# A decoder trunk's attention: quotients of two query tiles together, rotary addition on GpSimd, four PSUM banks for the cross attentions' last sums

## The chip, the cores and the metric

The kernel runs on one core of a Trainium2 chip. The metric is the device time of one execution in microseconds (us), the median of several runs.

## The reference

The program is two layers of a decoder trunk on 512 tokens of width 1024, in float32. In the stages that the change touches the reference computes:

```python
def diff_attention(x, ...):                 # layer 0: 8 heads
    q, k, v = split(x @ w_qkv, 3)           # per head two queries and two keys of 64, a value of 128
    q, k = rope(q), rope(k)
    lam = exp(sum(lq[0] * lk[0])) - exp(sum(lq[1] * lk[1])) + lam_init
    s = (q @ k.T) * 64 ** -0.5              # two score maps per head, causal mask
    p = softmax(where(mask, s, min))
    a = p[0] - lam * p[1]
    o = a @ v
    o = o * rsqrt(mean(o * o) + eps) * subln_g * (1 - lam_init)
    return o.reshape(S, H * 128) @ w_o
...
x = layer_norm(alpha * x + diff_attention(x, ...))
x = layer_norm(alpha * x + memory_cross_attention(x, mem, wq, wkv, wo))
```

Each layer is: a half-step SwiGLU network, a token mixer (layer 0: differential attention; layer 1: a pooling mixer), cross attention with 4 heads to 256 memory tokens, and a second SwiGLU network, each followed by a layer norm. In `rope` the halves of a head are rotated: x1 · cos − x2 · sin and x2 · cos + x1 · sin.

## The kernel before, in words

Every large product is made as three products of a float32 value's rounded part and rest (`mm3`, L201 to L203, named hi·hi, hi·lo and lo·hi here). To split a tile, ScalarE copies the rounded part (L114, tiles named `wh`, `a`, `xh`) and VectorE subtracts it (L115, `wl`, `a`, `xl`). PSUM has pairs of banks: `mm` for projections and last sums (`self.mm`), and `px`, `py`, `yz`, which `self.aux` takes in turn unless a pair is named. A bank comes free when the last reader has read it.

**The differential attention** (layer 0) is two programs that run woven into each other. `da_main` makes for each of the 8 heads the query and key projections (and values for two heads at once), and after each projection `da_rope` (L947 to L953): a shuffle of the projection on VectorE (L949), a product with the cosine on VectorE (L950), a product with the signed sine on GpSimd (L951), and the addition of both on VectorE (L952). Then the query is split (L962 ScalarE, L963 VectorE), or the key (L976 and L978 ScalarE, L977 VectorE). `da_side` goes through 32 steps, 8 heads by 4 query tiles of 128. Step s makes the scores of its tile, transposes the map of step s − 2, multiplies the map of step s − 3 with the values, and after a head's last tile scales and transposes the output. `weave` hands `da_side` a turn for each GAP of 900 ns of projection matmuls and starts a head's scores only LEAD of 6000 ns after its key.

For query tile i of a head `da_scores` makes two score maps of 128 × 128(i + 1) on TensorE (L991, L992), adds the mask and finds the row bound on VectorE (L996), and takes the exponential on ScalarE with the row sums as a second output (L997, sums in `sd`). Then VectorE makes the reciprocal of the second sum (L1000, `rc`), the factor −lam · sum0 / sum1 (L1001, `cf`) and the combination p0 + cf · p1 (L1002), the *quotient* in this text. The map stays unnormalised; the row norm of the output takes the first sum in.

`da_turn` transposes the combined map on TensorE (L479, `pt`), and L114 and L115 split it to `a`. `da_out` multiplies `a` with the values (L1022, L1023); every second tile ScalarE copies one half of the sum (L1027), VectorE adds the other (L1028), and ScalarE sums the squares of the two tiles (L1031). After a head's last tile GpSimd makes the row factor `f`: two small products of the first sums (L1038, L1039), the sum of squares added (L1040), and a power of −0.5 (L1041). ScalarE scales the four output tiles by it (L1047).

**The end of a cross attention** is `to_tokens`: 8 sums of 128 × 512 (`ps`, 4 heads' parts, L201 to L203) in the order `LAST`, each in the next of the two `mm` banks. VectorE adds each to the residual (L397) and so frees the bank. After a token tile's second half `ln_token` makes the layer norm: the mean (L406), the squares on ScalarE (L419), variance and its power on GpSimd (L420, L421), and two passes on VectorE (L423, L425); `turn_late` then transposes the tile for the next stage (L479) in between the last sums.

The order of the instructions on each engine is not written out. The program's scheduler lays it down ahead of the run, engine by engine, from the order of the calls and the data that they need; each engine then goes through its list and waits where an input or a buffer is missing.

Of the kernel before, what the change touches and what calls it, by code (L numbers as in the profile page):

```python
# [13 lines left out]
ALU = mybir.AluOpType  # L14
# [3 lines left out]
P = 128  # L18
D = 1024
S = 512  # L20
NT = S // P
# [5 lines left out]
ALPHA = (2 * DEPTH) ** 0.25  # L27
# [72 lines left out]
def drain(units):  # L100
    for _ in units:
        pass


class Trunk:
# [375 lines left out]

    def to_tokens(self, parts, w, k0, kn, first, last, scale, homes=(None, None)):

        nc = self.nc
        ws = [None, None]
        for half, t in LAST if last else sorted(LAST):
            c, o = slice(half * S, (half + 1) * S), slice(t * P, (t + 1) * P)
            if t == 0:
                ws[half] = self.rows(w, k0, kn, half * S, homes[half])
            ps = self.mm("ps")  # L490
            for k in range(kn):
# [454 lines left out]
    def da_rope(self, ps):  # L946
        nc = self.nc  # L947
        t1, t2 = self.tmp("rt"), self.tmp("rt")
        nc.vector.stream_shuffle(t2, ps, [(i + 16) % 32 for i in range(32)])  # L949
        nc.vector.tensor_tensor(t1, ps, self.ropeC, ALU.mult)  # L950
        nc.gpsimd.tensor_tensor(t2, t2, self.ropeS, ALU.mult)  # L951
        nc.vector.tensor_tensor(t1, t1, t2, ALU.add)  # L952
        return t1  # L953
# [27 lines left out]
    def da_scores(self, st, i):  # L981
# [3 lines left out]
        qi, kn = slice(i * P, n), slice(0, n)  # L985
        mx, rc, cf = self.small("mx"), self.small("rc", (P, 1)), self.small("cf", (P, 1))
        sm = st["sm"][:, i]
# [6 lines left out]
        for m in range(2):  # L994
# [4 lines left out]
            )  # L999
        nc.vector.reciprocal(rc, sm[:, 1:2])  # L1000
        nc.vector.scalar_tensor_tensor(cf, sm[:, 0:1], self.nlam, rc, ALU.mult, ALU.mult)  # L1001
        nc.vector.scalar_tensor_tensor(p[0], p[1], cf, p[0], ALU.mult, ALU.add)  # L1002
        st["p", i] = p[0]

# [72 lines left out]
    def da_side(self):  # L1077
# [4 lines left out]
        self.nc.sync.dma_start(self.mask[:, S - P :], self.a["mask"])  # L1082
        for s in range(n + LS + 2):
            h, i = divmod(s, NT)
            if s < n:
# [314 lines left out]
    def xa(self, layer, ln):  # L1400
# [6 lines left out]
        homes = [[lambda: self.pair("q")] * 4, [kv] * 4]  # L1407
        drain(self.to_tokens(self.oT[4:], self.a["xa_wo"][layer], 4, 4, False, True, ALPHA, homes))

# [69 lines left out]
    def mixer(self, layer, ln):  # L1479
        if layer == 0:  # L1480
            bufs = dict(low=4, rt=2, a=4, p=4, o=1, qk=8, _x=0, v=4, oT=11, mask=1)
            with self.other_pools(), self.phase_pool(("v", "v"), "rt", **bufs):
# [60 lines left out]
```

## Time and profile before

| | |
|---|---|
| runs | 1938.06, 1935.68, 1937.65 us |
| median | 1937.65 us |
| the profiled execution | 1939.3 us |
| its span, first to last instruction | 1937.5 us |
| granted TensorE clock in it | 0.999 |
| instructions | 32405 |
| read from and written to memory | 274.15 MB, 4.20 MB |

In the profile PE is TensorE's matmul and PEld its weight load, DVE is VectorE, ACT ScalarE, POOL GpSimd. A row of the timeline has the start and the duration of an instruction in us, its engine and line, what it writes and reads, and in brackets the idle time of the engine before it and what ended it. A row of the waits has the total, the number and the longest of all waits of one kind. A row of the groups has the total us and the mean ns of one instruction, then the idle time just before them. The differential attention's woven part lies between about 375 and 560 us, the last sums of layer 0's cross attention around 735 to 756 us.

### The profile page before, as it was taken

To read this page: it belongs to the slowest core of one execution; us is meant where nothing else is said; L and a number is where in the kernel's file an instruction comes from. 1 tells how busy PE (TensorE), PEld (TensorE's weight loads), DVE (VectorE), ACT (ScalarE), POOL (GpSimd) and SP (SyncE) were. 2 spreads that over 40 slices of the span, in tenths; PEclk is the share of its full clock that TensorE was granted. 3 is DMA by queue.
4 is the path that set the end of the run, shared out by engine and by line. 5 is a ranking of instruction groups with operands and counts; after the bars stand their busy time and mean duration, and the time that the engine had idled before them with its cause. 6 is when DMAs were issued, how large, how long until landed. Compare 5 with 4: busy or idle time off the path is not lost.

```text
span 1937.5 us, 32405 instructions
## 1 busy us (share of the span) xinstructions
PE 1904.6 (98%) x12988; PEld 1738.8 (90%) x12988; DVE 1555.8 (80%) x2262; ACT 1015.8 (52%) x1543; POOL 334.8 (17%) x318
## 2 busy tenths in 40 slices
PE   9999999999999999999999999999999999999998
PEld 8999998888888888999998999999898889999996
DVE  7988887888867558788888988898886568898886
ACT  6655553567755435645554655455454436555552
POOL 2212121111211002211220321212110013211211
PEclk9999999999999999999999999999999999999999
DMA  9878772322126326978784688877444337777861
GB/s 253 198 173 185 171 145 66 92 67 87 56 97 196 109 66 153 218 175 163 141 193 135 114 203 174 178 161 164 142 153 141 109 87 122 190 174 168 187 140 44
DMA packets 254199, 280.46 MB, mean 145 GB/s; under 512 B 9184, under 2 KB 221792, under 8 KB 254048
## 3 DMA queue, kind: packets, MB, share of 16 engines
q0 software_dynamic: 95808, 102.77, 32.6%
q1 hardware_dynamic: 158240, 175.61, 28.6%
q8 instruction: 102, 1.67, 0.3%
q14 instruction: 49, 0.40, 0.1%
HBM read 274.15 MB, written 4.20 MB: 144 GB/s over the span
## 4 chain that ended last, share of the span: by engine, by line
PE 70%; DVE 17%; ACT 4%; DMA 4%; issue 2%; POOL 2%; SPq 0%; DVEq 0%; POOLq 0%; ACTq 0%
PE x L202 6%; PE x L201 6%; PE x L203 6%; PE z L202 4%; PE z L201 4%; PE z L203 4%; DVE wl L115 4%; PE ps L203 3%; PE ps L202 3%; DMA ra<-in_ffn_w_in_dram 3%; PE ps L201 3%; PE px L201 2%; PE px L203 2%; PE px L202 2%; PE xq L202 2%
## 5 line engine op out<-in xcount | busy, mean ns | idle before, releaser
L636 POOL DMA_DIRECT2D ra<-in_ffn_w_in_dram x132 | 170.4, 1315 | 988.3 <-DVE wl L115 971.4
L114 ACT CAST wh<-ra 128x1024 fp32r<-128x1024 f32 x184 | 193.3, 1053 | 209.1 <-PE x L202 56.0
L115 DVE TENSOR_TENSOR wl<-ra,wh 128x1024 fp32r<-128x1024 f32 x184 | 224.0, 1223 | 68.0 <-ACT wh L114 67.2
L114 ACT CAST wh<-rc 128x1024 fp32r<-128x1024 f32 x136 | 142.8, 1052 | 117.7 <-PE x L202 42.5
L201 PE MATMUL x<-xe,wh 128*128 128x256 f32 x704 | 195.6, 278 | 1.6 <-ACT sp L697 1.6
L201 PE MATMUL x<-xh,wh 128*128 128x256 f32 x704 | 196.0, 278 | 0.7 <-ACT xh L114 0.7
L202 PE MATMUL x<-xl,wh 128*128 128x256 f32 x704 | 195.6, 278 | 0.3 <-DVE xl L115 0.3
L203 PE MATMUL x<-xh,wl 128*128 128x256 f32 x704 | 195.6, 278 | 0.4 <-DVE wl L115 0.4
L202 PE MATMUL x<-xe,wh 128*128 128x256 f32 x704 | 195.3, 277 | 0.0
L203 PE MATMUL x<-xe,wl 128*128 128x256 f32 x704 | 195.3, 277 | 0.0
L114 ACT CAST wh<-b 128x1024 fp32r<-128x1024 f32 x112 | 117.8, 1051 | 128.6 <-PE x L202 63.2
L115 DVE TENSOR_TENSOR wl<-rc,wh 128x1024 fp32r<-128x1024 f32 x136 | 164.9, 1222 | 23.2 <-ACT wh L114 23.2
L115 DVE TENSOR_TENSOR wl<-b,wh 128x1024 fp32r<-128x1024 f32 x112 | 137.0, 1224 | 41.1 <-ACT wh L114 41.1
L201 PEld LDWEIGHTS x<-xe,wh 128*128 128x128 f32 x704 | 132.5, 188 | 3.2 <-ACT sp L697 1.8
L202 PEld LDWEIGHTS x<-xl,wh 128*128 128x128 f32 x704 | 132.7, 188 | 2.1 <-DVE xl L115 0.8
L201 PEld LDWEIGHTS x<-xh,wh 128*128 128x128 f32 x704 | 132.3, 188 | 2.2 <-ACT xh L114 0.9
L202 PEld LDWEIGHTS x<-xe,wh 128*128 128x128 f32 x704 | 132.5, 188 | 1.4
L203 PEld LDWEIGHTS x<-xh,wl 128*128 128x128 f32 x704 | 132.3, 188 | 0.6 <-DVE wl L115 0.6
L203 PEld LDWEIGHTS x<-xe,wl 128*128 128x128 f32 x704 | 132.4, 188 | 0.0
L203 PE MATMUL y<-xh,wl 128*128 128x256 f32 x352 | 98.8, 281 | 2.1 <-DVE wl L115 1.2
L201 PE MATMUL y<-xh,wh 128*128 128x256 f32 x352 | 98.1, 279 | 0.2 <-ACT wh L114 0.2
L202 PE MATMUL z<-xe,wh 128*128 128x256 f32 x352 | 97.8, 278 | 0.3 <-DVE xe L115 0.3
(401 smaller groups left out, 6056.0 us busy)
## 6 DMA issues: line engine op xcount, KB each, us to landing
ra<-in_ffn_w_in_dram POOLq DMA_DIRECT2D x132, 512.0 KB, 6.9
rc<-in_ffn_w_in_dram SPq DMA_DIRECT2D x88, 512.0 KB, 6.1
b<-in_ffn_w_out_dram SPq DMA_DIRECT2D x60, 512.0 KB, 5.0
ra<-in_ffn_w_in_dram SPq DMA_DIRECT2D x44, 512.0 KB, 5.0
rc<-in_ffn_w_in_dram POOLq DMA_DIRECT2D x44, 512.0 KB, 7.2
b<-in_ffn_w_out_dram POOLq DMA_DIRECT2D x16, 512.0 KB, 12.6
raw<-in_da_w_qkv_dram SPq DMA_DIRECT2D x16, 512.0 KB, 5.1
raw<-in_xa_wkv_dram SPq DMA_DIRECT2D x8, 1024.0 KB, 5.5
```

Of the source, the lines that this page charges most:

```text
L114: self.nc.scalar.copy(hi, src),
L115: self.nc.vector.tensor_sub(lo, src, hi.bitcast(F32)),
L201: mm(out, w[0], x[0], start=start, stop=False, skip_group_check=again)
L202: mm(out, w[0], x[1], start=False, stop=False, skip_group_check=again)
L203: self.last_mm = mm(out, w[1], x[0], start=False, stop=stop, skip_group_check=again)
L636: self.last_more = nc.gpsimd.dma_start(t, source(*block), accum_op=ALU.add)
```

## The change

Three edits, and the buffers for them. The quotients of tiles i − 1 and i are made together, in a new function `da_maps`, with one reciprocal and one factor of 128 × 2; it is called for every odd tile i at the start of the step after its scores. So that the maps last longer, `p` gets 6 buffers where it had 4. The rotary embedding's last addition goes from VectorE to GpSimd. And the cross attentions' last `to_tokens` puts every second sum in a bank of `yz`.

```diff
@@ -479,15 +479,15 @@
             self.nc.tensor.transpose(pt[:, j], b, self.ident)
 
 
-    def to_tokens(self, parts, w, k0, kn, first, last, scale, homes=(None, None)):
+    def to_tokens(self, parts, w, k0, kn, first, last, scale, homes=(None, None), spare=None):
 
         nc = self.nc
         ws = [None, None]
-        for half, t in LAST if last else sorted(LAST):
+        for n, (half, t) in enumerate(LAST if last else sorted(LAST)):
             c, o = slice(half * S, (half + 1) * S), slice(t * P, (t + 1) * P)
             if t == 0:
                 ws[half] = self.rows(w, k0, kn, half * S, homes[half])
-            ps = self.mm("ps")
+            ps = self.aux("ps", spare) if spare and n % 2 else self.mm("ps")
             for k in range(kn):
                 h = parts[k]
                 yield self.mm3(ps, (h[0][:, o], h[1][:, o]), ws[half][k], k == 0, k == kn - 1)
@@ -949,7 +949,7 @@
         nc.vector.stream_shuffle(t2, ps, [(i + 16) % 32 for i in range(32)])
         nc.vector.tensor_tensor(t1, ps, self.ropeC, ALU.mult)
         nc.gpsimd.tensor_tensor(t2, t2, self.ropeS, ALU.mult)
-        nc.vector.tensor_tensor(t1, t1, t2, ALU.add)
+        nc.gpsimd.tensor_tensor(t1, t1, t2, ALU.add)
         return t1
 
     def da_query(self, ps):
@@ -983,7 +983,7 @@
         nc = self.nc
         q, k, n = st["q"], st["k"], (i + 1) * P
         qi, kn = slice(i * P, n), slice(0, n)
-        mx, rc, cf = self.small("mx"), self.small("rc", (P, 1)), self.small("cf", (P, 1))
+        mx = self.small("mx")
         sm = st["sm"][:, i]
         sc = [self.aux("sc")[:, :n] for m in range(2)]
         mm = nc.tensor.matmul
@@ -997,10 +997,18 @@
             nc.scalar.activation(
                 p[m], p[m], AF.Exp, bias=top, scale=-1.0, accum_out=sm[:, m : m + 1]
             )
-        nc.vector.reciprocal(rc, sm[:, 1:2])
-        nc.vector.scalar_tensor_tensor(cf, sm[:, 0:1], self.nlam, rc, ALU.mult, ALU.mult)
-        nc.vector.scalar_tensor_tensor(p[0], p[1], cf, p[0], ALU.mult, ALU.add)
-        st["p", i] = p[0]
+        st["ps", i] = p
+
+    def da_maps(self, st, i):
+
+        nc = self.nc
+        rc, cf, s2 = self.small("rc"), self.small("cf"), st["sm"][:, i - 1 : i + 1]
+        nc.vector.reciprocal(rc, s2[:, :, 1])
+        nc.vector.scalar_tensor_tensor(cf, s2[:, :, 0], self.nlam, rc, ALU.mult, ALU.mult)
+        for n in range(2):
+            p = st.pop(("ps", i - 1 + n))
+            nc.vector.scalar_tensor_tensor(p[0], p[1], cf[:, n : n + 1], p[0], ALU.mult, ALU.add)
+            st["p", i - 1 + n] = p[0]
 
     def da_turn(self, st, i):
         pt = self.aux("pt").rearrange("p (c n) -> p c n", c=NT)
@@ -1081,6 +1089,9 @@
         self.nc.gpsimd.memset(self.mask[:, : S - P], 0.0)
         self.nc.sync.dma_start(self.mask[:, S - P :], self.a["mask"])
         for s in range(n + LS + 2):
+            h, i = divmod(s - 1, NT)
+            if 0 < s <= n and i % 2:
+                self.da_maps(self.heads[h][1], i)
             h, i = divmod(s, NT)
             if s < n:
                 while h >= len(self.heads) or self.clock < self.heads[h][0] + LEAD:
@@ -1405,7 +1416,8 @@
         self.begin_ln(layer, ln, 1.0)
         kv = lambda: tuple(self.kvp.tile([P, S], F32R, tag="kv", name="kv", bufs=8) for _ in range(2))
         homes = [[lambda: self.pair("q")] * 4, [kv] * 4]
-        drain(self.to_tokens(self.oT[4:], self.a["xa_wo"][layer], 4, 4, False, True, ALPHA, homes))
+        wo = self.a["xa_wo"][layer]
+        drain(self.to_tokens(self.oT[4:], wo, 4, 4, False, True, ALPHA, homes, "yz"))
 
 
     def run(self):
@@ -1478,7 +1490,7 @@
 
     def mixer(self, layer, ln):
         if layer == 0:
-            bufs = dict(low=4, rt=2, a=4, p=4, o=1, qk=8, _x=0, v=4, oT=11, mask=1)
+            bufs = dict(low=4, rt=2, a=4, p=6, o=1, qk=8, _x=0, v=4, oT=11, mask=1)
             with self.other_pools(), self.phase_pool(("v", "v"), "rt", **bufs):
                 self.diff_attention(layer, ln)
             self.close_side()
```

In the new kernel the reciprocal, factor and quotient are L1006, L1007 and L1010, the row factor is L1046 to L1049, the copy, addition and squares of the output L1035, L1036 and L1039, the scaling L1055.

How the lists of the engines move is shown at two places. A row has the line, the operation, the tile written, the tiles read and the shape; the numbers behind the names only tell tiles apart and differ between the programs.

The first place is head 4, from its last score tile (512 wide) on, while the query of head 6 is rotated. ScalarE's list before: `p_5458` and `p_5459` are the two maps of head 4's last tile, `o_5208` the output of head 3, `f_5438` its row factor, `qk` the query of head 6.

```order
L997 ACTIVATE p_5458,sd_5198<-p_5458,mx_5449 128x512
L997 ACTIVATE p_5459,sd_5198<-p_5459,mx_5449 128x512
L1047 ACTIVATE o_5208<-o_5208,f_5438 128x128
L114 CAST a_5497<-pt_5494 128x256
L1047 ACTIVATE o_5208<-o_5208,f_5438 128x128 x3
L962 ACTIVATE qk_5473<-rt_5467 64x512
L962 ACTIVATE qk_5474<-rt_5467 64x512
```

ScalarE's list after, where these are `p_5415`, `p_5416`, `o_5170` and `f_5397`:

```order
L1039 ACTIVATE po_5341,sq_5171<-o_5170 128x128
L1055 ACTIVATE o_5170<-o_5170,f_5397 128x128
L997 ACTIVATE p_5415,sd_5160<-p_5415,mx_5408 128x512
L997 ACTIVATE p_5416,sd_5160<-p_5416,mx_5408 128x512
L1055 ACTIVATE o_5170<-o_5170,f_5397 128x128
L962 ACTIVATE qk_5427<-rt_5421 64x512
L962 ACTIVATE qk_5428<-rt_5421 64x512
L114 CAST a_5451<-pt_5448 128x256
```

The first scaling of the output stood behind both exponentials of the tile and stands ahead of them now. The query's copies and the split of the transposed map have changed places.

VectorE's list at the same place before, from the cosine product of the query on. `rt_5467` is the rotated query of head 6, `rc_5450` and `cf_5451` belong to the last tile, `a_5498` is a split of a transposed map. The quotient of the third tile (384 wide, `p_5402`) stands before these rows, ahead of the query's shuffle.

```order
L950 TENSOR_TENSOR rt_5467<-q_5362,ropeC_655 128x512
L115 TENSOR_TENSOR wl_5786<-raw_5779,wh_5785 128x1024
L1000 RECIPROCAL rc_5450<-sd_5198 128x1
L952 TENSOR_TENSOR rt_5467<-rt_5467,rt_5468 128x512
L1001 SCALAR_TENSOR_TENSOR cf_5451<-sd_5198,nlam_3834,rc_5450 128x1
L115 TENSOR_TENSOR a_5498<-pt_5494,a_5497 128x256
L1002 SCALAR_TENSOR_TENSOR p_5458<-p_5459,cf_5451,p_5458 128x512
L963 SCALAR_TENSOR_TENSOR qk_5473<-rt_5467,qk_5473 64x512
L963 SCALAR_TENSOR_TENSOR qk_5474<-rt_5467,qk_5474 64x512
```

VectorE's list after, from the cosine product of the query (`rt_5421`) on:

```order
L950 TENSOR_TENSOR rt_5421<-q_5320,ropeC_655 128x512
L115 TENSOR_TENSOR wl_5732<-raw_5725,wh_5731 128x1024
L1006 RECIPROCAL rc_5470<-sd_5160 128x2
L1007 SCALAR_TENSOR_TENSOR cf_5471<-sd_5160,nlam_3834,rc_5470 128x2
L963 SCALAR_TENSOR_TENSOR qk_5427<-rt_5421,qk_5427 64x512
L963 SCALAR_TENSOR_TENSOR qk_5428<-rt_5421,qk_5428 64x512
L115 TENSOR_TENSOR a_5452<-pt_5448,a_5451 128x256
L1010 SCALAR_TENSOR_TENSOR p_5364<-p_5365,cf_5471,p_5364 128x384
L1010 SCALAR_TENSOR_TENSOR p_5415<-p_5416,cf_5471,p_5415 128x512
```

The quotient of the third tile stood ahead of the query's shuffle. It stands behind the query's two L963 and the split of the transposed map now, directly ahead of the quotient of the last tile, and the addition L952 is no longer in the list.

GpSimd's list at this place before, the sine product of head 6's query first and that of its key last:

```order
L951 TENSOR_TENSOR rt_5468<-rt_5468,ropeS_656 128x512
L1040 TENSOR_TENSOR f_5438<-f_5438,sq_5209 128x4
L1041 TENSOR_TENSOR f_5438<-f_5438,mhalf_84 128x4
L1038 TENSOR_SCALAR f_5707<-sd_5198 128x4
L1039 TENSOR_TENSOR f_5707<-f_5707,sd_5198 128x4
L951 TENSOR_TENSOR rt_5560<-rt_5560,ropeS_656 128x512
```

GpSimd's list after:

```order
L951 TENSOR_TENSOR rt_5422<-rt_5422,ropeS_656 128x512
L1048 TENSOR_TENSOR f_5397<-f_5397,sq_5171 128x4
L1049 TENSOR_TENSOR f_5397<-f_5397,mhalf_84 128x4
L1046 TENSOR_SCALAR f_5658<-sd_5160 128x4
L1047 TENSOR_TENSOR f_5658<-f_5658,sd_5160 128x4
L952 TENSOR_TENSOR rt_5421<-rt_5421,rt_5422 128x512
L951 TENSOR_TENSOR rt_5515<-rt_5515,ropeS_656 128x512
L952 TENSOR_TENSOR rt_5514<-rt_5514,rt_5515 128x512
```

The query's addition (L952) has come in behind the power of head 3's row factor (L1049) and behind the first two products of head 4's (L1046, L1047); the key's follows its sine product.

The second place is head 2's key. VectorE's list before, from the query's addition (L952) to the key's shuffle (L949):

```order
L952 TENSOR_TENSOR rt_4537<-rt_4537,rt_4538 128x512
L1001 SCALAR_TENSOR_TENSOR cf_4521<-sd_4223,nlam_3834,rc_4520 128x1
L115 TENSOR_TENSOR a_4568<-pt_4564,a_4567 128x256
L1002 SCALAR_TENSOR_TENSOR p_4528<-p_4529,cf_4521,p_4528 128x512
L963 SCALAR_TENSOR_TENSOR qk_4543<-rt_4537,qk_4543 64x512
L963 SCALAR_TENSOR_TENSOR qk_4544<-rt_4537,qk_4544 64x512
L949 STREAM_SHUFFLE rt_4596<-k_4549 128x512
```

VectorE's list after, between the same steps (the query's addition is no longer in it):

```order
L1006 RECIPROCAL rc_4564<-sd_4214 128x2
L1007 SCALAR_TENSOR_TENSOR cf_4565<-sd_4214,nlam_3834,rc_4564 128x2
L963 SCALAR_TENSOR_TENSOR qk_4521<-rt_4515,qk_4521 64x512
L963 SCALAR_TENSOR_TENSOR qk_4522<-rt_4515,qk_4522 64x512
L115 TENSOR_TENSOR a_4546<-pt_4542,a_4545 128x256
L1010 SCALAR_TENSOR_TENSOR p_4458<-p_4459,cf_4565,p_4458 128x384
L1010 SCALAR_TENSOR_TENSOR p_4509<-p_4510,cf_4565,p_4509 128x512
L949 STREAM_SHUFFLE rt_4580<-k_4527 128x512
```

`rt_4537` and `rt_4515` are the rotated query of head 2, `p_4528` and `p_4509` the last map of head 1. The split `a` and the quotient stood ahead of the query's L963; now they stand behind it, with the quotient of the third tile (`p_4458`) between them, and all three are ahead of the key's shuffle.

## The prediction

> **What bounds the kernel now.** I read the totals, then the window of the differential attention, its waits, its groups of instructions, and last the timeline at single places. The page's totals:
> ```profile
> PE 1904.6 (98%) x12988; PEld 1738.8 (90%) x12988; DVE 1555.8 (80%) x2262; ACT 1015.8 (52%) x1543; POOL 334.8 (17%) x318
> ```
> Of the span of 1937.5 us TensorE leaves about 33 us idle (1937.5 − 1904.6). The change touches no matmul, so it can win only a piece of those 33 us, or add to them. The window table over the attention (its length, then busy time of PE, PEld, DVE, ACT, POOL):
> ```profile
> 375.00:560.00 185.00, 180.29 (x1086) 157.46 (x1085) 161.49 (x412) 128.55 (x346) 32.22 (x44) 1.00 0.23 70
> ```
> Here only 4.7 us are idle on TensorE, at the full clock; VectorE is busy 87% and GpSimd 17%. Nothing an engine other than TensorE saves here can be worth more than those 4.7 us. The waits of that window (waiting, releaser: total us, times, longest):
> ```profile
> DVE rc L1000 <- ACT p L997: 15.2, 17, 2.6
> ...
> ACT o L1047 <- POOL f L1041: 11.2, 8, 2.3
> ...
> PE sc L991 <- DVE a L115: 3.6, 4, 2.5
> ```
> VectorE idles 15.2 us for the exponentials, ScalarE 11.2 us for GpSimd's power, and TensorE only 3.6 us for the split of a transposed map, whose PSUM bank the next scores need. What decides is when TensorE gets its inputs, not how much VectorE has to do. The groups (total us, mean ns):
> ```profile
> L951 POOL TENSOR_TENSOR rt<-rt,ropeS 128x512 f32<-128x512 f32 x16 | 20.9, 1304 | 108.6 <-DVE rt L949 108.6
> ...
> L1047 ACT ACTIVATE o<-o,f 128x128 f32<-128x128 f32 x32 | 11.1, 394 | 11.2 <-POOL f L1041 11.2
> L963 DVE SCALAR_TENSOR_TENSOR qk<-rt,qk 64x512 fp32r<-64x512 f32 x16 | 11.0, 686 | 1.5 <-ACT qk L962 1.0
> L952 DVE TENSOR_TENSOR rt<-rt 128x512 f32<-128x512 f32 x16 | 10.9, 679 | 0.1
> ...
> L996 DVE CUSTOM_DVE_ANT_0 p<-sc,mask 128x384 f32<-128x384 f32 x16 | 8.3, 552 | 0.2
> ...
> L1001 DVE SCALAR_TENSOR_TENSOR cf<-sd,nlam,rc 128x1 f32<-128x1 f32 x32 | 6.9, 216 | 0.6
> ...
> L1002 DVE SCALAR_TENSOR_TENSOR p<-p,cf 128x512 f32<-128x512 f32 x8 | 6.2, 779 | 0.1
> ...
> L1000 DVE RECIPROCAL rc<-sd 128x1 f32<-128x1 f32 x32 | 5.2, 162 | 15.4 <-ACT p L997 15.2
> ```
>
> **The change part by part.** VectorE loses 16 additions of .679 (10.9 us) and half of its reciprocals and factors, 16 × (.162 + .216) = 6.0 us. GpSimd gains 16 additions; the nearest row is the same shape there, the product L951: 1.304 each, twice VectorE's .679, and I take that. Against this, the first map of each pair must wait for the exponentials of the second. In most of the 16 pairs TensorE transposes the first map so late that this costs nothing; what hides it is the projection's matmuls that stand between, and where they are few I go place by place. On GpSimd the addition waits for VectorE's cosine product; behind it there stand the next product and the next output's row factors, which ScalarE's scalings wait for, and in this stage the loads are issued by SyncE, whose queue is not passed.
>
> *Head 0, first tile.* Timeline (start, length):
> ```profile
> 381.58 0.50 ACT L997 ACTIVATE p<-p,mx 128x256 f32<-128x256 f32 x1
> 381.71 0.35 DVE L1002 SCALAR_TENSOR_TENSOR p<-p,cf 128x128 f32<-128x128 f32 x1
> ...
> 382.12 0.33 PE L479 MATMUL pt<-ident,p 128*128 128x128 f32 x1
> ```
> The quotient ends at 382.06 and TensorE takes it at 382.12: no slack. Now it starts only after the second tile's exponential (382.08): .16 + .22 + .35 = .73 later, and up to 1.5 if reductions of the third tile (.55 each) get between. I take **+1.2**.
>
> *Head 2, its key.*
> ```profile
> 411.05 0.42 DVE L115 TENSOR_TENSOR a<-pt,a 128x256 fp32r<-128x256 f32 x1
> ...
> 413.49 0.73 DVE L949 STREAM_SHUFFLE rt<-k 128x512 f32<-128x512 f32 x1
> ...
> 416.07 0.68 DVE L952 TENSOR_TENSOR rt<-rt 128x512 f32<-128x512 f32 x1
> ...
> 418.07 1.27 ACT L978 CAST qk<-qk 64x512 fp32r<-64x512 f32 x2
> ...
> 419.58 0.27 PE L991 MATMUL sc<-qk 128*128 128x128 f32 x1
> ```
> The key's last copies end at 419.34, .24 before the scores. In the new order VectorE has a split (.42), the quotients of 384 (.61, row below) and of 512 (.78) behind the query's L963 and ahead of the key's shuffle; L963 can't come sooner, as its input's copies already follow the addition at once. So the shuffle is 1.81 later. The addition grows by .62, but the .54 that it waits today behind a weight split (413.49 + .73 + 1.30 to 416.07) goes. 1.81 + .08 − .24 = **+1.7** (0 if ScalarE's earlier work catches up, 1.9 at most).
>
> *Head 4, its key.*
> ```profile
> 458.27 1.43 POOL L1041 TENSOR_TENSOR f<-f,mhalf 128x4 f32<-128x4 f32 x1
> ...
> 458.47 0.71 ACT L997 ACTIVATE p<-p,mx 128x512 f32<-128x512 f32 x1
> ...
> 463.19 0.68 DVE L952 TENSOR_TENSOR rt<-rt 128x512 f32<-128x512 f32 x1
> ...
> 466.50 0.33 PE L991 MATMUL sc<-qk 128*128 128x128 f32 x1 [0.20 <-ACT qk L978]
> ```
> Here a new wait is added: ScalarE's order puts the first scaling of the outputs, which waits for GpSimd's power, ahead of both exponentials. 458.27 + 1.43 + .39 + 2 × .71 = 461.5, where they end at 459.2 today. Behind that stand on VectorE the pair's reciprocal and factor and then the key's shuffle: 461.5 + .16 + .22 + .73, product 1.30, addition 1.30 = 465.2; today the addition ends at 463.9. The scores already wait for this key, so it is **+1.4** (.95 to 1.5).
>
> *Head 4, third tile.*
> ```profile
> 483.59 0.61 DVE L1002 SCALAR_TENSOR_TENSOR p<-p,cf 128x384 f32<-128x384 f32 x1
> ...
> 486.21 0.71 ACT L997 ACTIVATE p<-p,mx 128x512 f32<-128x512 f32 x1
> ...
> 486.57 2.12 POOL L1041 TENSOR_TENSOR f<-f,mhalf 128x4 f32<-128x4 f32 x1
> ...
> 488.75 0.49 PE L479 MATMUL pt<-ident,p 128*128 128x128 f32 x3
> ...
> 495.04 0.36 PE L991 MATMUL sc<-qk 128*128 128x256 f32 x1 [2.46 <-DVE a L115]
> ```
> Today the quotient is done 4.5 us ahead of the transposes. Now ScalarE's scaling, and both of the partner's exponentials behind it, wait for the power: it ends at 488.0 if it takes the 1.43 of head 4's key, at 488.7 if 2.12 as here. Then on ScalarE a scaling, two exponentials, a scaling and the query's two copies (.39 + 1.42 + .39 + 1.26, the copies as the key's), on VectorE the second L963 (.69), the split of 256 (.42) and the quotient of 384 (.61): ready at 493.2 to 493.9. TensorE has 495.04 − 488.75 − 2.46 = 3.8 us of work from there to the scores at 495.04, and its present wait of 2.46 is used up: 497.0 to 497.7, that is 2.0 to 2.7 late. GpSimd's addition, 1.30 behind the power, ends by about the time that the copies begin and isn't counted. I take the lower half, **+2.1**, since VectorE has more time before it.
>
> *Head 5, third tile.*
> ```profile
> 511.94 0.49 PE L479 MATMUL pt<-ident,p 128*128 128x128 f32 x3
> ...
> 512.76 0.71 ACT L997 ACTIVATE p<-p,mx 128x512 f32<-128x512 f32 x1
> ...
> 513.87 0.38 PE L1022 MATMUL po<-v,a 128*128 128x256 f32 x1 [0.37 <-ACT a L114]
> ...
> 517.21 0.39 PE L991 MATMUL sc<-qk 128*128 128x256 f32 x1 [0.17 <-DVE a L115]
> ```
> Today TensorE transposes this map before the partner's exponential has begun. The quotient now ends at 512.76 + .71 + .16 + .22 + .61 = 514.5 at the earliest, 515.1 with the next head's two reductions (128 wide, some .3 each) in between: 2.5 to 3.2 late, of which the waits of .37 and .17 take .5. The squares now stand ahead of the query's copies on ScalarE, so the power and that exponential may come .6 earlier. 1.4 to 2.7; I take **+1.7**.
>
> *What goes.* The other TensorE waits for that split are 3.6 − 2.46 − .17 = 1.0, and I credit them whole: **−1.0**. In the cross attention of layer 0 two more banks remove one wait:
> ```profile
> 745.34 0.50 PE L201 MATMUL ps<-kv,oT 128*128 128x512 f32 x1 [1.25 <-DVE X L397]
> ...
> 750.19 1.28 DVE L425 SCALAR_TENSOR_TENSOR X<-X,rstd,gb 128x1024 f32<-128x1024 f32 x1
> ...
> 751.84 1.03 PE L479 MATMUL pt<-ident,X 128*128 128x128 f32 x8
> ```
> It is 1.25 us, but then TensorE comes sooner to the transposes at 751.84, and their input ends at 751.47: only .37 of the 1.25 is left, **−.4**. The Trainium skill, "Perfetto Trace Analysis", section Matmuls, says that independent groups should rotate through different PSUM banks so that one's evacuation overlaps the next's matmuls; by that the whole 1.25 would be won, and by the rows the normalisation on VectorE is late next. Layer 1 shows no such wait: 0. The two more buffers for p move no work.
>
> The sum is 1.2 + 1.7 + 1.4 + 2.1 + 1.7 − 1.0 − .4 = **+6.7 us**. The profiled execution took 1939.3, so 1946.0; the median of the runs is 1.65 below that, inside .1%, and from it the time is 1937.65 + 6.7 = 1944.4.
>
> *An unknown on VectorE.*
> ```profile
> 504.51 1.30 POOL L951 TENSOR_TENSOR rt<-rt,ropeS 128x512 f32<-128x512 f32 x1 [8.82 <-DVE rt L949]
> 504.85 2.04 DVE L115 TENSOR_TENSOR wl<-raw,wh 128x1024 fp32r<-128x1024 f32 x1
> ```
> The page has the same split at:
> ```profile
> L115 DVE TENSOR_TENSOR wl<-rc,wh 128x1024 fp32r<-128x1024 f32 x136 | 164.9, 1222 | 23.2 <-ACT wh L114 23.2
> ```
> Beside a GpSimd product it took .82 longer. Sixteen more GpSimd operations may so give back between 0 and 16 × .82 = 13.1 us of the 10.9 saved; most of it would fall into VectorE's idle time, so it is only in the upper end of the range. The Trainium skill, "SBUF — State Buffer", section Who interferes with whom, says that a VectorE instruction with two SBUF inputs contends with a GpSimd instruction that reads SBUF, and that the one issued second is blocked until the other ends. The row agrees: 2.04 − 1.22 leaves the split starting its work at 505.67, close to the product's end at 505.81.
>
> **The rivals.** *Faster, .15.* VectorE's relief reaches TensorE. If VectorE runs ahead by a part of its 16.9 us, the pair waits fall into idle time, and the bank waits go: −3.6 − .4 = −4.0, so 1933.7. It decides at head 4: the second exponential would have to be over by 487.7 for the quotient to meet 488.75, and today it is over at 486.9. Against it: the new order puts the scaling, and so the power's end at 488.7, ahead of both exponentials. *About the same, .23.* The terms don't add, since a late TensorE lets the other engines catch up for the next place. Only the largest (2.1) and one key (1.4) stay, less 1.4: +2.1, 1939.8. For it: VectorE has 23.5 us idle in the window. *Worse, .12.* Powers stay slow (2.12) and splits blocked beside additions: the upper ends, 1.5 + 1.9 + 1.5 + 2.7 + 2.7 = 10.3 without the reliefs, 1947.9. That the change doesn't do what it says is true of layer 1's four banks, and costs nothing.
>
> **How the numbers follow.** The forecast has .50; its own range, from all lower ends less 1.4 to all upper ends less 1.4, is +3.7 to +8.9, 1941.3 to 1946.5. The whole range goes from 1936.0 (both reliefs, no new wait: −1.4) to 1949.5 (the worse case and 1.6 more for blocked splits). .2% is 3.9 us, about what a measurement of this kernel can tell from no change. Slower by more: the forecast and the worse case, .62; same .23; faster .15.
>
> **What would show it.** In the new profile: TensorE waits before transposes of p behind the quotient line, at head 4 (about 4 us beyond 488.75) and head 5; the wait at 495.04 gone; the GpSimd addition near 1.3 us; scores of heads 2 and 4 waiting for L978's copies; four banks saving about .4 in layer 0. It is wrong if TensorE's busy share in the attention rises, if exponentials precede the scaling in time at heads 4 and 5, or if transposes don't wait.

## The result, and the profile after

| | median | runs |
|---|---|---|
| before | 1938.06 us | 5 (1935.68 to 1938.78) |
| after | 1960.3 us | 5 (1957.19 to 1961.72) |
| ratio | 1.0115 | 95% interval 1.0101 to 1.0128 |

The changed kernel is 22 us slower. The forecast was 1944.4, 6.7 us slower, with a range up to 1949.5: the direction was right, the size a third of the measured one. The totals of the changed kernel's page:

```profile
PE 1914.3 (98%) x12988; PEld 1747.0 (89%) x12988; DVE 1552.4 (79%) x2214; ACT 1018.3 (52%) x1543; POOL 356.4 (18%) x334
```

TensorE has the same number of matmuls, 9.7 us more busy, and the span is 20.2 us longer. When the same matmul is looked up in both traces, it has fallen back by 19.6 us more at the end of the differential attention than at its beginning, and by hardly more at any place behind it. The window of the attention, which now ends near 580 (length, busy PE, PEld, DVE, ACT, POOL, then the granted clock):

```profile
375.00:580.00 205.00, 189.72 (x1087) 164.87 (x1086) 159.27 (x369) 131.72 (x348) 52.82 (x58) 0.95 0.21 65
```

VectorE is busy 159.3 of 205 us, 78%, where it was 87%. It was relieved, and the time became idle time: TensorE idles 15.3 us here against 4.7. The clock of 0.95 is new, too. The waits of 375 to 590 in the new trace:

```profile
DVE rc L1006 <- ACT p L997: 14.3, 13, 2.9
ACT qk L976 <- POOL rt L952: 13.1, 7, 4.2
...
ACT qk L962 <- POOL rt L952: 11.2, 6, 3.4
PE pt L479 <- DVE p L1010: 10.6, 6, 3.0
ACT o L1055 <- POOL f L1049: 10.5, 7, 2.3
...
PE sc L991 <- ACT qk L978: 2.8, 4, 1.3
...
PE sc L991 <- DVE a L115: 1.9, 1, 1.9
```

and before, 375 to 566, ScalarE's waits for the rotation:

```profile
ACT qk L962 <- DVE rt L952: 9.1, 5, 2.7
ACT qk L976 <- DVE rt L952: 8.8, 6, 3.2
```

(`...` stands for rows that are left out.) TensorE's new waits are 10.6 us for the quotients and 2.8 for the last copies of keys. ScalarE waits 24.3 us for the rotated tile instead of 17.9. The groups between 340 and 600 us, after:

```profile
L310 DVE TENSOR_TENSOR wl<-raw,wh 128x512 fp32r<-128x512 f32 x32 | 30.5, 980 | 4.1 <-ACT wh L308 3.8
L952 POOL TENSOR_TENSOR rt<-rt 128x512 f32<-128x512 f32 x16 | 26.5, 1655 | 2.4 <-DVE rt L950 0.9 <-DVE rc L1006 0.6
```

and before:

```profile
L310 DVE TENSOR_TENSOR wl<-raw,wh 128x512 fp32r<-128x512 f32 x32 | 24.2, 769 | 4.0 <-ACT wh L308 3.7
```

The addition takes 1.655 us on GpSimd, not the 1.304 that was reckoned, and VectorE's weight splits beside it went from .769 to .980.

At head 4's third tile the chain ran as the prediction told it. The timeline of the changed kernel there:

```profile
497.97 1.04 POOL L1049 TENSOR_TENSOR f<-f,mhalf 128x4 f32<-128x4 f32 x1
...
499.04 0.40 ACT L1055 ACTIVATE o<-o,f 128x128 f32<-128x128 f32 x1 [2.25 <-POOL f L1049]
499.35 0.71 ACT L997 ACTIVATE p<-p,mx 128x512 f32<-128x512 f32 x1
...
500.06 0.71 ACT L997 ACTIVATE p<-p,mx 128x512 f32<-128x512 f32 x1
...
500.70 1.28 POOL L952 TENSOR_TENSOR rt<-rt 128x512 f32<-128x512 f32 x1
...
501.09 0.91 DVE L1007 SCALAR_TENSOR_TENSOR cf<-sd,nlam,rc 128x2 f32<-128x2 f32 x1
...
502.01 1.28 ACT L962 ACTIVATE qk<-rt 64x512 fp32r<-64x512 f32 x2 [0.86 <-POOL rt L952]
502.67 1.40 DVE L963 SCALAR_TENSOR_TENSOR qk<-rt,qk 64x512 fp32r<-64x512 f32 x2 [0.67 <-ACT qk L962]
...
504.11 0.42 DVE L115 TENSOR_TENSOR a<-pt,a 128x256 fp32r<-128x256 f32 x1
504.45 1.27 DVE L1010 SCALAR_TENSOR_TENSOR p<-p,cf 128x384 f32<-128x384 f32 x2
...
505.12 0.90 PE L479 MATMUL pt<-ident,p 128*128 128x128 f32 x3 [2.88 <-DVE p L1010]
```

Power, scaling, two exponentials, copies, L963, split, quotient: each waits for the one before, and TensorE waits 2.88 us at the end. Two things were not reckoned with: the factor L1007 took .91 instead of .22, since GpSimd's addition (500.70 to 501.98) runs beside it, and the query's copies do wait for that addition (.86). Behind the wait the clock drops. Windows of 2 us:

```profile
502.00:504.00 2.00, 0.23 (x1) 0.00 (x0) 1.29 (x2) 1.91 (x4) 0.00 (x0) 1.00 0.87 336
504.00:506.00 2.00, 0.89 (x4) 0.89 (x5) 1.97 (x7) 0.44 (x3) 0.00 (x0) 0.60 0.00 0
506.00:508.00 2.00, 2.00 (x9) 1.71 (x8) 0.80 (x5) 2.00 (x6) 0.00 (x0) 0.50 0.04 8
508.00:510.00 2.00, 2.00 (x9) 1.60 (x8) 2.00 (x4) 0.15 (x1) 1.69 (x2) 0.50 0.00 0
```

Until 511 TensorE runs at half the clock; so it does behind four other waits of this trace, for 3.4 us each.

### The profile page after: what moved, and what is told of

Read it like the earlier page. It is cut to its first block, busy times and chain, and to the rows that moved or that the text cites. A ratio compares the mean times of both kernels' runs of the same rounds, so it can differ in the third digit from the quotient of the medians.

```text
span 1957.7 us, 32365 instructions
## 1 busy us (share of the span) xinstructions
PE 1914.3 (98%) x12988; PEld 1747.0 (89%) x12988; DVE 1552.4 (79%) x2214; ACT 1018.3 (52%) x1543; POOL 356.4 (18%) x334
## 4 chain that ended last, share of the span: by engine, by line
PE 70%; DVE 15%; ACT 5%; DMA 4%; POOL 3%; issue 2%; SPq 0%; POOLq 0%; DVEq 0%; ACTq 0%
PE x L202 6%; PE x L201 6%; PE x L203 6%; PE z L202 4%; PE z L201 4%; PE z L203 4%; DVE wl L115 3%; PE ps L203 3%; PE ps L202 3%; PE ps L201 3%; DMA ra<-in_ffn_w_in_dram 3%; PE px L201 2%; PE px L203 2%; PE px L202 2%; PE xq L202 2%
```

## The experiments

All times are medians beside the runs of the kernel before on the same chip; the ratio has its 95% interval.

**The three parts, each alone.** The pairs (`da_maps` and six buffers for `p`, without the other two edits):

> The kernel before with the paired quotients (and six buffers for p) alone; the addition stays on VectorE, two banks. Theory 1 (each pair that comes late makes TensorE wait, and a wait of some 2 us or more is followed by a stretch at half the granted clock, .5 for 3 to 6 us): waits for the quotients at heads 0, 4 and 5, one or two stretches at .5; slower than before by 8 to 14 us. Rival (the pairs alone cost only their waits, at full clock, and the rest is the addition's doing): slower by 3 to 6 us, granted clock 1.0 throughout the attention.

1947.03 against 1939.76 us, ratio 1.0032 (1.0020 to 1.0044). The addition:

```diff
-        nc.vector.tensor_tensor(t1, t1, t2, ALU.add)
+        nc.gpsimd.tensor_tensor(t1, t1, t2, ALU.add)
```

> The kernel before with the rotary addition on GpSimd alone. Theory 1: the quotients are where they were, only keys come later by .6 to 1 us; waits under 2 us, hardly a stretch at half clock: slower by 2 to 6 us. Rival (GpSimd and VectorE hold each other up, additions of 1.6 to 2.2 us against the 1.3 reckoned, and that makes most of the loss): slower by 8 to 14 us, with waits behind the key's copies at several heads.

1958.7 against 1939.76 us, 1.0094 (1.0082 to 1.0107). The banks (`spare` in `to_tokens`):

> The kernel before with the four banks alone. Theory 1: the wait of 1.25 us for a bank in layer 0 goes, and comes back at the transposes of X behind it: within 1 us of before. Rival (the banks are worth their wait): faster by 1.2 us.

1938.08 against 1939.76 us, 0.9993 (0.9984 to 1.0002).

So the addition makes 18.9 us of it, the pairs 7.3, and the banks nothing that can be told; together 24.5, against 22.2 for all three. The first theory, in which the pairs were the greater part, fell with these runs. The rival for the addition has the right part, but 18.9 us is more than its 8 to 14; the 7.3 us of the pairs lie between the two ranges given for them, and their trace has one stretch at half the clock. In the trace with the addition alone, two instructions show what GpSimd's work does to VectorE's:

```profile
519.05 1.73 DVE L1002 SCALAR_TENSOR_TENSOR p<-p,cf 128x384 f32<-128x384 f32 x1
519.07 1.30 POOL L952 TENSOR_TENSOR rt<-rt 128x512 f32<-128x512 f32 x1
```

A quotient of this size takes .615 us in the mean of before; here it takes 1.1 us more. And the waits of that trace, 360 to 590:

```profile
ACT qk L976 <- POOL rt L952: 21.4, 8, 3.8
...
ACT qk L962 <- POOL rt L952: 14.5, 7, 3.5
```

The banks did what the prediction said: the wait at 745.34 went, and TensorE came to the transposes of X too early. The trace with the banks alone:

```profile
749.85 1.29 DVE L425 SCALAR_TENSOR_TENSOR X<-X,rstd,gb 128x1024 f32<-128x1024 f32 x1
751.19 1.10 PE L479 MATMUL pt<-ident,X 128*128 128x128 f32 x8 [0.95 <-DVE X L425]
```

A wait of .95 stands here that before had not. Of 1.6 us gained at the bank 1.0 is given back here.

**The clock.** Is the half clock behind the waits a cost of its own? Fillers in `da_turn`, ahead of three transposes:

```diff
         p = st.pop(("p", i))
+        if (st["h"], i) in ((0, 0), (4, 2), (5, 2)):
+            x = self.xh[0]
+            for _ in range(11):
+                self.nc.tensor.matmul(pt.rearrange("p c n -> p (c n)"), x[:, 0, :P], x[:, 0, :], start=True, stop=True)
```

> The changed kernel with 11 matmuls of 128x512 on data that is there, ahead of the transposes of the three maps that waited about 3 us (head 0 tile 1 of 4, head 4 and head 5 tile 3 of 4), into the same bank, which the transposes then write over; the result is the same. Theory 1 (half of the loss is the clock after a wait): the fillers run within the wait, 2.4 us each, the clock stays at 1.0 behind them, where the changed kernel has .5 for 3.6, 6.3 and 3.6 us: 1.8 + 3.1 + 1.8 = 6.7 us faster than the changed kernel, about 1953.5. Rival (the slow stretch has another cause, such as late weights): the stretches stay, no change against the changed kernel, 1960.

1962.39 against 1939.76 us, 1.0123 (1.0102 to 1.0144): no better than the changed kernel's 1.0115. The fillers did their part. At head 4's third tile, windows of 2 us:

```profile
509.00:511.00 2.00, 0.84 (x5) 0.77 (x6) 1.97 (x7) 0.46 (x2) 0.00 (x0) 1.00 0.00 0
511.00:513.00 2.00, 2.00 (x14) 1.76 (x13) 0.90 (x5) 1.99 (x6) 0.00 (x0) 1.00 0.00 0
```

The clock stays at 1.00 and TensorE catches up 2.8 us on the changed kernel from here to the next scores; but then it waits 1.29 and .73 us for VectorE. Over the attention the clock cost 10.2 us of TensorE in the changed kernel (one less the granted clock, summed over 10 us windows) and 1.7 with the fillers, and the kernel is no faster. So keeping the clock up wins nothing here; that the half clock costs nothing is not shown, since the fillers also move other engines' lists. At head 0 the split of the first map stands later in ScalarE's list, and TensorE waits 1.95 us for it (at 393.34), which it doesn't in the changed kernel. (The profiled execution took 1973.31 us; some 10 us of that were lost between 1400 and 1600 us, far from this stage.)

**What the addition costs: late, or in the way?** Two kernels leave the addition on VectorE and change next to nothing but GpSimd's list. In one GpSimd does a second addition behind each product, into a buffer `ru` that nobody reads:

```diff
         nc.gpsimd.tensor_tensor(t2, t2, self.ropeS, ALU.mult)
+        nc.gpsimd.tensor_tensor(self.tmp("ru"), t2, self.ropeS, ALU.add)
```

> The kernel before, with the addition on VectorE as it was, and on GpSimd behind each of the 16 sine products a further addition of the same shape into a tile that nobody reads. The lists of TensorE and VectorE are those of before. Theory 2 (the moved addition costs by blocking: VectorE's two-input instructions wait while GpSimd's runs, as the quotient of 1.73 us beside the addition at 519.07 in the run with the addition alone): 8 to 14 us slower. Rival A (it costs by being late itself): 0 to 3 us slower. Rival B (it costs by the lists that the scheduler lays down anew): the same, 0 to 3 us, since the lists stay.

1953.96 against 1939.13 us, 1.0078 (1.0063 to 1.0093). This one holds up VectorE's own addition too (1.24 us in place of .68), so it is late and in the way at once; 14.8 us is a little over the range for blocking. In the other four small products make the rotated tile late:

```diff
         nc.gpsimd.tensor_tensor(t2, t2, self.ropeS, ALU.mult)
+        for _ in range(4):
+            nc.gpsimd.tensor_scalar(t2[:, :4], t2[:, :4], 1.0, None, ALU.mult)
```

> The kernel before, with four products of 128x4 by one on GpSimd between the sine product and VectorE's addition, which thereby is some 1.1 us later, with hardly any data read on GpSimd; all of the lists but GpSimd's are those of before. Theory 2 (blocking): 0 to 4 us slower. Rival A (lateness: the rotated tile reaches ScalarE's copies later, and what is queued behind them on ScalarE waits too): 8 to 16 us slower. Rival B (new lists): 0 to 4 us.

1952.17 against 1939.13 us, 1.0066 (1.0052 to 1.0080). Its groups: the small products read 128x4, and VectorE's addition keeps its .69 us.

```profile
L953 POOL TENSOR_SCALAR rt<-rt 128x4 f32<-128x4 f32 x64 | 20.1, 313 | 5.1
...
L954 DVE TENSOR_TENSOR rt<-rt 128x512 f32<-128x512 f32 x16 | 11.1, 692 | 12.9 <-POOL rt L953 12.8
```

The same with two in place of four:

> As the run with four small products on GpSimd ahead of VectorE's addition, with two of them: the addition's input is some .6 us later, all lists but GpSimd's as before. Lateness at every rotation (each us of it is paid at most of the 16): about half of that run's 13 us, 5 to 8 us slower. Rival (a slack of some half a microsecond hides it, and only what lies beyond costs): 0 to 3 us slower.

1947.2 against 1939.0 us, 1.0041 (1.0028 to 1.0053). Lateness alone costs, and from the first half microsecond on. Measured from the start of the shuffle to the end of the addition, mean of the 16 rotations in each trace: 3.89 us before, 4.35 with two small products (8.2 us slower), 4.85 with four (13.0 slower), 4.42 with the addition on GpSimd (18.9 slower). The smaller delay costs a little more than the 5 to 8 us expected. It isn't paid alike at each rotation. In the trace with four small products TensorE falls back by 13.5 us over the attention: 2.5 at head 0's first transposes, 4.2 around head 2's key, 2.8 at head 4's key, and nothing at head 7's query and key. By the medians, lateness of the size that the addition has makes about half of the 18.9. For the rest, GpSimd's extra addition was put behind VectorE's, where it delays no rotation:

```diff
         nc.vector.tensor_tensor(t1, t1, t2, ALU.add)
+        nc.gpsimd.tensor_tensor(self.tmp("ru"), t1, self.ropeS, ALU.add)
```

> The kernel before, with an addition of 128x512 on GpSimd behind VectorE's addition of each rotation, into a tile that nobody reads: nothing waits for it, all lists but GpSimd's are those of before, and it runs beside whatever VectorE does next. If VectorE's being held up by GpSimd counts by itself: 4 to 10 us slower. Rival (only the rotation's lateness counts): within 2 us of before.

1952.67 against 1939.18 us, 1.0072 (1.0059 to 1.0085). The rotation takes 3.89 us as before, nothing waits for the new instruction, and it still costs 13.5 us. The groups show where it is paid, in VectorE's two-input instructions beside it:

```profile
L310 DVE TENSOR_TENSOR wl<-raw,wh 128x512 fp32r<-128x512 f32 x32 | 27.8, 883 | 5.2 <-ACT wh L308 5.2
L953 POOL TENSOR_TENSOR ru<-rt,ropeS 128x512 f32<-128x512 f32 x16 | 22.2, 1390 | 23.6 <-DVE rt L952 23.5
...
L978 DVE TENSOR_TENSOR low<-rt,qk 64x512 fp32r<-64x512 f32 x16 | 15.1, 941 | 0.5
...
L1003 DVE SCALAR_TENSOR_TENSOR p<-p,cf 128x384 f32<-128x384 f32 x8 | 7.3, 917 | 0.1
```

and before:

```profile
L977 DVE TENSOR_TENSOR low<-rt,qk 64x512 fp32r<-64x512 f32 x16 | 10.9, 684 | 0.5
...
L1002 DVE SCALAR_TENSOR_TENSOR p<-p,cf 128x384 f32<-128x384 f32 x8 | 4.9, 615 | 0.1
```

L978 takes .941 for .684, L310 .883 for .769, and the quotients (L1003) of 384 take .917 for .615: 4.1, 3.6 and 2.4 us more. Summed over the attention, VectorE's instructions last 12.4 us longer than the same ones before, ScalarE's no longer, and TensorE falls back by 12.3 us. GpSimd's longer list is not the way: ScalarE's scalings wait 10.2 us for the row factor, 11.2 before. The range for blocking, 4 to 10 us, was too low. Last, the two steps exchanged, product on VectorE and addition on GpSimd:

```diff
-        nc.gpsimd.tensor_tensor(t2, t2, self.ropeS, ALU.mult)
-        nc.vector.tensor_tensor(t1, t1, t2, ALU.add)
+        nc.vector.tensor_tensor(t2, t2, self.ropeS, ALU.mult)
+        nc.gpsimd.tensor_tensor(t1, t1, t2, ALU.add)
```

> The kernel before with the two last steps of the rotation exchanged: the sine product on VectorE, the addition on GpSimd. GpSimd has 16 instructions of 128x512 and VectorE as many as before. If GpSimd's extra work counts (blocking): within 3 us of before. Rival (a last step on GpSimd, and the lists that the scheduler lays down for it, count): 6 to 15 us slower.

1946.56 against 1939.18 us, 1.0044 (1.0031 to 1.0058). The rotation takes 4.44 us, and the loss is that of a rotation so late (8.2 at 4.35): the new lists of this kernel add nothing that shows. Without more work on GpSimd, the addition there costs 7.4 us; with it 18.9.

The lists of the kernel with the addition alone are others, and there they count. ScalarE at head 7's key, before:

```profile
515.55 0.47 ACT L114 CAST a<-pt 128x384 fp32r<-128x384 f32 x1
...
516.30 1.26 ACT L976 CAST qk<-rt 64x512 fp32r<-64x512 f32 x2 [0.28 <-DVE rt L952]
```

and with the addition alone:

```profile
530.83 1.26 ACT L976 CAST qk<-rt 64x512 fp32r<-64x512 f32 x2 [1.78 <-POOL rt L952]
...
534.18 0.46 ACT L114 CAST a<-pt 128x384 fp32r<-128x384 f32 x1
...
535.28 0.58 PE L991 MATMUL sc<-qk 128*128 128x256 f32 x1 [4.27 <-DVE a L115]
```

The split of the transposed map stood ahead of the key's copies. Now it stands behind them and behind two exponentials, so it waits for the addition too, and TensorE, which waited .17 us for this split, waits 4.27; the half clock follows. From here to the end of the attention TensorE falls back by 6.2 of its 18.5 us. The kernels with small products, with a second addition, and with the two steps exchanged keep the split ahead of the copies and lose at most .9 us here. So the 18.9 us have three parts: the late rotation, VectorE held up, and this new order. They overlap and are not priced apart, since no run has the old lists with the addition on GpSimd. In the changed kernel the split stands behind the copies, too, but TensorE doesn't wait for it; there the third part doesn't show.

**Keys and queries.** The addition on GpSimd for keys alone, and for queries alone (`da_rope` gets the engine from its caller):

> The kernel before with the addition on GpSimd for the 8 keys alone, on VectorE for the 8 queries. Theory 2 (blocking): about half of the 18.9 us, 8 to 11. Rival A (lateness): more than half, 11 to 16, as a head's first scores wait for the key's last copies and the query is ready long before. Rival B: between 3 and 15, as the lists fall.

1950.77 against 1939.13 us, 1.0058 (1.0046 to 1.0070).

> The kernel before with the addition on GpSimd for the 8 queries alone. The keys alone cost 11.6 us and both 18.9. If the two add up: 5 to 9 us slower. Rival (either one delays the same chain on ScalarE, and the second adds little): 9 to 14 us slower.

1947.12 against 1939.0 us, 1.0042 (1.0027 to 1.0058). 11.6 + 8.1 = 19.7 against 18.9: the costs add up. With the keys alone ScalarE has the new order at head 7's key too, with the same wait of 4.27 us; TensorE falls back by 6.8 us there, more than half of what it loses in that trace's attention (11.6).

**The other way round.** The whole rotation on VectorE:

```diff
-        nc.gpsimd.tensor_tensor(t2, t2, self.ropeS, ALU.mult)
+        nc.vector.tensor_tensor(t2, t2, self.ropeS, ALU.mult)
```

> The kernel before with the sine product on VectorE too, so that the whole rotation is there: 16 times .68 = 10.9 us more work for VectorE, 20.9 less for GpSimd, and the rotated tile ready about .6 us sooner if VectorE is free. If lateness counts both ways: 3 to 8 us faster. If VectorE's work counts (the reason given for the change): 4 to 10 us slower. If both, or neither: within 3 us.

1939.91 against 1939.0 us, 1.0003 (0.9992 to 1.0013). VectorE got 16 instructions more (10.9 us), the rotation takes 4.03 us, and the time didn't change. But VectorE's busy time grew by 2.9 us only (1555.8 to 1558.7), since its weight splits no longer run beside GpSimd's product (L310 .685 us in place of .769). More work and less holding up came out even; that VectorE's amount of work doesn't count is not shown.

**Where the pairs cost.** Without the three pairs that the prediction named for quotients (first of head 0, second of heads 4 and 5):

```diff
+ALONE = ((0, 0), (4, 1), (5, 1))
...
-            if 0 < s <= n and i % 2:
+            if 0 < s <= n and i % 2 and (h, i // 2) not in ALONE:
```

> The kernel before with paired quotients (p in six buffers) in 13 of the 16 pairs; the first pair of head 0 and the second pairs of heads 4 and 5 are made tile by tile as before. Theory 1 (the loss of the pairs, 7 us, is the wait at the few places where the first map is transposed soon): 0 to 3 us slower. Rival (the pairs shift the lists everywhere): 5 to 8 us slower still.

1944.94 against 1939.13 us, 1.0032 (1.0019 to 1.0044): 5.8 us against 7.3 with all pairs, a difference within the intervals, and more than the 0 to 3 us expected of waits at these three places. TensorE's waits for quotients, 360 to 600, with all pairs and with these 13:

```profile
PE pt L479 <- DVE p L1010: 7.1, 7, 3.1
```
```profile
PE pt L480 <- DVE p L1021: 3.8, 4, 2.1
```

(In the second kernel the lines are shifted; L480 and L1021 are the transposes and the quotients.) The remaining waits stand at the first pairs of head 2 (.72), head 4 (.73) and head 5 (2.08). The last was .27 with all pairs, so it moves with the lists. With these three left out as well, `ALONE = ((0, 0), (2, 0), (4, 0), (4, 1), (5, 0), (5, 1))`:

> The kernel before with paired quotients in 10 of the 16 pairs; those at which TensorE was seen to wait for a quotient with all pairs, or with 13 (heads 0, 2, 4 and 5 first pair, heads 4 and 5 second pair), are made tile by tile. If the pairs cost by those places: within 2 us of before. Rival (they cost by the lists that are laid down anew): 4 to 7 us slower.

1941.04 against 1939.0 us, 1.0009 (0.9998 to 1.0020). Ten pairs cost nothing that can be told, and bring nothing. No version tried beats the kernel before by more than can be told from no change.

## Why the prediction came out as it did

**What bounds the kernel** was half right. That relief of VectorE would bring nothing fits the result: VectorE idles more, and TensorE is no sooner done. But the prediction took VectorE's 23.5 us of idle time for room, and so for cover. Most of it is none: VectorE is idle while it waits for ScalarE (15.2 us for the exponentials before), and ScalarE waits for the rotation or for VectorE's reductions. What lasts longer on VectorE so comes back to TensorE at many places, not only where TensorE waits today: 12.4 us more on VectorE cost 12.3 us with GpSimd's useless addition. Not at all places: at head 7's rotations the delay of the small products cost nothing.

**The addition on GpSimd** is where the sum failed: of its 6.7 us this part is .7 at most (.08 at head 2 and .62 at head 4), and it costs 18.9 us alone and 15.0 on top of the pairs (22.2 − 7.3, the banks with it). First, 1.30 us and twice VectorE's time was about right for an addition that runs alone, but its lateness was priced at two keys only, as .08 us at head 2 and as a part of 1.4 us at head 4, on the ground that TensorE waits there. It is paid at more places than those: .46 us more per rotation cost 8.2 us. Second, blocking was written down (0 to 13.1 us), and set aside with the words that "most of it would fall into VectorE's idle time". Blocking alone cost 13.5 us. Of the 16.9 us that VectorE was to be spared, its busy time shows 3.4 (1555.8 to 1552.4); L310's splits alone last 6.3 us longer (24.2 to 30.5). The new order at head 7's key is a part of the 18.9 us, but not of the changed kernel's loss. The worse rival, with its chance of .12, named blocking too, but came to 10.3 us in all, with 1.6 more for blocked splits at the end of the range. Lateness and blocking together are more (8.2 + 13.5) than the 18.9 of the addition; how they and the new order overlap was not separated.

The Trainium skill's rule in "SBUF — State Buffer", section Who interferes with whom, spoke against this edit, and the runs agree with it: VectorE's two-input instructions last longer beside GpSimd's (1.73 for .61), and the small products, which read only 128x4, hardly touched the weight splits (.779 for .769).

**The places, one by one.** *Head 0, first tile*: +1.2 was forecast. In the changed kernel TensorE waits 2.85 us there, with the pairs alone .9: the pairs' part is within the .73 to 1.5 given, and the rest is lost ahead of it, where the reductions stand behind weight splits on VectorE that GpSimd's addition held up. *Head 2's key*: +1.7 forecast, and in the new trace

```profile
423.19 1.26 ACT L976 CAST qk<-rt 64x512 fp32r<-64x512 f32 x2 [4.21 <-POOL rt L952]
...
425.14 0.33 PE L991 MATMUL sc<-qk 128*128 128x128 f32 x1 [1.29 <-ACT qk L978]
```

TensorE waits 1.29 here; its matmuls fall back by 1.5 us. The size was right and the cause wrong: with the pairs alone they fall back by .4 at this place, with the addition alone by 1.6. *Head 4's key*: 1.4 forecast (its own times give 465.2 − 463.9 = 1.3), 1.2 seen; again 1.3 with the addition alone, and nothing lost with the pairs alone. So the new order of the quotients and of the scaling, to which these two terms were mostly put down, cost next to nothing here. *Head 4, third tile*: 2.1 net forecast; TensorE falls back by 3.0 at the transposes and gains 2.6 where the wait of 2.46 was, and at half clock it loses 2.7 in between: in the changed kernel the mechanism and its links were as told, the clock was missing. With the pairs alone TensorE falls back by 1.3 only at these transposes and gains the same 2.6, so here, too, the loss needs the addition. *Head 5, third tile*: 2.5 to 3.2 us late forecast, and here

```profile
526.92 0.71 ACT L997 ACTIVATE p<-p,mx 128x512 f32<-128x512 f32 x1
...
530.58 1.27 DVE L1010 SCALAR_TENSOR_TENSOR p<-p,cf 128x384 f32<-128x384 f32 x2
...
531.25 0.55 PE L479 MATMUL pt<-ident,p 128*128 128x128 f32 x3 [2.98 <-DVE p L1010]
```

2.98 us (3.07 with the pairs alone). The net loss is 3.4 us, not 1.7, since TensorE runs at half clock behind the wait. *In most of the 16 pairs this costs nothing*: ten cost nothing that can be told. At three of the other six, the first pairs of heads 2, 4 and 5, TensorE waits too, and the prediction doesn't name them. All of the forecast but the addition's .7 and the banks' −.4 was put down to the pairs, 6.4 us at least; the pairs alone cost 7.3. That total is near by luck, since the places differ: nothing is lost at head 4's key with the pairs alone.

**The banks** were right: of the wait that goes only a part is left, and the interval of the run reaches from 3.1 us faster to .4 slower. The rule of the Trainium skill's "Perfetto Trace Analysis", section Matmuls, holds in that the wait for the bank went; that all of it would be won, the trace does not show, since X is late next (.95).

**The faster rival** needed VectorE's relief to reach TensorE. The test that it named, at head 4, went against it as told: the exponentials stand behind the power.

## What to carry to other kernels

Idle time of an engine is cover only if the engine isn't waiting for work that the delayed step feeds; read what the idle engine waits for before hiding anything under it. Moving an instruction to a slower engine is to be priced at each place where it stands, as lateness of what comes next and as time taken from the engines that it holds up, not only at the places where the bounding engine waits today. A cheap test of both, ahead of the change: leave all as it is and add a useless instruction on the slow engine, once ahead of the step that waits and once behind it. What the test can't show is the new order that a scheduler gives the other lists once the edit is real; compare the lists all through the stage, not at two places.

## What the runs showed of the hardware

TensorE's granted clock fell to 0.50 for 3.4 us, once for 6.8, behind waits of 1.3 to 3.0 us in the changed kernel; in the kernel before a wait of 2.46 us at 495.04 left it at 1.00. The length of the wait alone doesn't decide.

GpSimd's useless addition behind VectorE's holds one instruction of VectorE each time: 16 additions, 16 instructions (L310, L978, L1003 and one L964), 12.3 us longer in all. Each of them reads two tiles in SBUF, begins .05 to .85 us behind the start of the addition beside it, and ends .28 to .55 us behind its end. A split of a transposed map, one of whose inputs lies in PSUM, is not held: at 418.92 it runs beside the addition and takes .42 us as before. In the kernel with the addition alone one held instruction is recorded .02 us ahead of GpSimd's: the quotient at 519.05 ends at 520.78, .41 us behind the addition's end (519.07 + 1.30 = 520.37).
